# Recurrence by pairs of channel blocks, the merge's rows split behind its first gate, one lasting set of stream buffers, and no gather steps at three borders

## Chip, cores and metric

One core of a Trainium2 chip runs the whole program. The metric is the device time of one execution in microseconds (us); a smaller one is better.

## What is computed

One decoder layer for 512 prompt tokens and 8 x 4 sample tokens, 544 columns in all, 2048 channels, everything in float32:

```python
proj = rmsnorm(x) @ w_in                       # q, k, v, indexer, xb, yb, memory queries
o_attn = attend(top-k keys of an indexer)       # 8 heads
xc = conv_b + sum(shift(xb, j) * conv_w[j])     # width 4, per channel
r = sigmoid(xc_blk @ w_rg + b_rg); i = sigmoid(xc_blk @ w_ig + b_ig)   # 8 blocks of 128 channels
a = exp(-8 * r * softplus(-lam)); u = sqrt(1 - a*a) * (i * xc)
h[t] = a[t] * h[t-1] + u[t]; o_lru = h * gelu(yb)
o_mem = attend(256 memory tokens)               # 4 heads
x = x + sum_n(sigmoid(xn @ w_gate[n]) * (o_n @ w_br[n])) @ w_o
x = x + PEER(rmsnorm(x))    # 16384 one-neuron experts: 8 heads, the best 16 of 128 x 128 keys each
y = rmsnorm(x)
```

## The kernel before, in words

**Matmuls in three parts.** Weights stay in DRAM and stream in chunks of 512 KB. `stream` (L239) loads one with a SyncE DMA (L242) into a buffer `raw`, ScalarE casts it to `hi` and VectorE forms `lo = raw - hi` (`split`, L221 to L223). `project` (L257) multiplies 8 k-blocks of a chunk as hi x hi, hi x lo and lo x hi: 48 matmuls of L272 for 16 k-blocks. The ring holds 3 buffers each of raw, hi and lo in pool `st`; `widen(stack, raw, hl, side)` (L230) opens a further pool with more of them for as long as that stack is open.

**Order.** The program is written out by hand; the build orders each engine's instructions by their place in it, those inside `urgent()` 3000 places ahead, among the ones it takes to be ready. Every engine, and SyncE with its DMAs, then works in that order. Side work is written as generators in four queues (`bg`, `bg2`, `bg3`, `bg4`). Each k-block of a projection calls `pump` once, which adds `rate / 8` steps to each queue's account and takes whole steps from its first generator up to the next `yield`. `drain` takes all that are left.

**Stages.** Prompt and sample tokens are worked off in two parts: part 0 has 288 columns (`xF`), part 1 has 256 (`xA`). `branches(part)` (L391) projects with `w_in` and runs attention heads (`bg2`), memory heads (`bg`) and the recurrence (`bg4`). `merge` (L926) follows, then `output_proj` (L968). Part 0 goes first; `pairs` (L1165) then finds the experts of its tokens, `branches(1)`, `merge`, `output_proj` and `pairs` follow for part 1, then `up` (L1316) for 128 blocks of experts, gate matrices (L1328) beside some of them, and `down` (L1453) with the remaining `up`s. All through this, `bg3` gathers single expert rows for 224 tokens by indirect DMAs on POOL (L1195) and works on them in VectorE (L1243, L1251): one step a row of 128 x 2048 floats, 448 rows, 472 steps in all.

**The recurrence.** `lru(c, xb, late)` (L738) handles block c of 8. Its yields: conv (POOL copies, 4 VectorE operations on part 1); the r gate (weights, matmul L766, sigmoid L768); the i gate; tanh (L773), exp (L775), two VectorE operations and sqrt (L778); the product on POOL (L780), VectorE and the scan (L792); and, once `late` holds the y-branch projection, gelu (L799), product (L800) and the store to `o_dram` (L801). Apart from the gate weights, with two, every tile of it has one buffer. L908 to L911 projects xb of block c, queues the generator, and projects yb. `staged` (L429) copies a projection into one of five `stage` buffers.

**Merge.** For each branch n (memory, attention, recurrence), 8 tiles of `o_dram` are loaded as `oraw` (L940) and split into `oh`, `ol` (L941); then 16 gates (L945) and, two behind, 16 branch projections (L953). `oraw` and the gates' sigmoids `sg` share four buffers of one tag. Gate results wait in PSUM (`ps_p`, four tiles).

**Memory.** SBUF is filled by two stacks, left and right. In part 1 the branch pools lie on the right, under `xA`: `keep` (kT, vN and others, 10.8 KiB a partition by its tiles' shapes), `stage` 5, `ap` 3.5, `lr` 9.1, `bc` (attention), `mp` (memory heads). At L1292 a set of two raw, hi and lo (24 KiB) is opened on the right in place of `keep`, `stage`, `ap` and part of `lr`; it is closed after the merge, opened anew at L1299 for `output_proj`, closed, and opened again at L1309 beside `rp2`. A tile placed on another one's memory waits until that is done with.

Of the kernel before, what the change touches and what calls it, by code (L numbers as in the profile page):

```python
# [176 lines left out]
def program(tc, ins, outs):  # L177
# [213 lines left out]
    def branches(part):  # L391
# [346 lines left out]
        def lru(c, xb, late):  # L738
            def v(i):
                return vec[:, i + c:i + c + 1]  # L740

            xp = lp.tile([128, 3 + HB], F, name="xp")
            if first:
                nc.gpsimd.memset(xp[:, :3], 0.0)
            else:
                nc.gpsimd.tensor_copy(xp[:, :3], tail[:, c])
            nc.gpsimd.tensor_copy(xp[:, 3:], xb[:, p0:])
            xc = lp.tile([128, n_], F, name="xc")
            convs = [(xc[:, p0:], lambda j: xp[:, j:j + HB])]
            if first:  # L750
                nc.gpsimd.tensor_copy(tail[:, c], xp[:, HB:])
                xs = lp.tile([128, NB, 3 + NT], F, name="xs")
                nc.gpsimd.tensor_copy(xs[:, :, :3], scv[:, c])
                nc.gpsimd.tensor_copy(xs[:, :, 3:], bt(xb))
                convs.append((bt(xc), lambda j: xs[:, :, j:j + NT]))
            for dst, src in convs:
                nc.vector.tensor_scalar(dst, src(0), v(V_CW), v(V_CB), op0=OP.mult, op1=OP.add)
                for j in range(1, 4):
                    nc.vector.scalar_tensor_tensor(dst, src(j), v(V_CW + 8 * j), dst, op0=OP.mult, op1=OP.add)
            yield  # L760
            gates = []
            for name, bcol in (("w_rg", V_BR), ("w_ig", V_BI)):
                w = lp.tile([128, 128], F, name=name, bufs=2)
                nc.sync.dma_start(w, ins[name][:, c])
                p = ps_w.tile([128, 512], F, name="w1")
                nc.tensor.matmul(p[:, :n_], w, xc, start=True, stop=True)  # L766
                g = lp.tile([128, n_], F, name=f"g{bcol}")
                nc.scalar.activation(g, p[:, :n_], AF.Sigmoid, bias=v(bcol))  # L768
                gates.append(g)
                yield  # L770
            rg, ig = gates
            th = lp.tile([128, n_], F, name="th")
            nc.scalar.activation(th, rg, AF.Tanh, scale=la[:, 1, c:c + 1])  # L773
            av = lp.tile([128, n_], F, name="av")
            nc.scalar.activation(av, rg, AF.Exp, scale=la[:, 0, c:c + 1])  # L775
            nc.vector.tensor_tensor(rg, av, av, op=OP.mult)
            nc.vector.scalar_tensor_tensor(th, rg, 1.0, th, op0=OP.add, op1=OP.mult)
            nc.scalar.activation(th, th, AF.Sqrt)  # L778
            yield
            nc.gpsimd.tensor_tensor(ig, ig, xc, op=OP.mult)  # L780
            nc.vector.tensor_tensor(th, th, ig, op=OP.mult)
            t0 = lp.tile([128, NB], F, name="t0")
            if first:
                nc.vector.tensor_tensor(t0, bt(av)[:, :, 0], slr[:, c], op=OP.mult)
                nc.vector.tensor_tensor(bt(th)[:, :, 0], bt(th)[:, :, 0], t0, op=OP.add)
                nc.vector.memset(av[:, 0:P0 + 1:NT], 0.0)
            else:
                nc.vector.tensor_tensor(t0[:, :1], av[:, :1], hl[:, c, 0:1], op=OP.mult)
                nc.vector.tensor_tensor(th[:, :1], th[:, :1], t0[:, :1], op=OP.add)
                nc.vector.memset(av[:, :1], 0.0)  # L790
            hs = lp.tile([128, n_], F, name="hs")
            nc.vector.tensor_tensor_scan(hs, av, th, 0.0, op0=OP.mult, op1=OP.add)  # L792
            nc.gpsimd.tensor_copy(hl[:, c, 0:1], hs[:, n_ - 1:])
            if first:
                nc.gpsimd.tensor_copy(hl[:, c, 1:], bt(hs)[:, :, NT - 1])
            yield
            while not late:
                yield
            nc.scalar.activation(ig, late[0], AF.Gelu_apprx_tanh)  # L799
            nc.vector.tensor_tensor(ig, hs, ig, op=OP.mult)  # L800
            nc.sync.dma_start(o_dram[8 + c, :, cols], ig)  # L801
            yield
# [98 lines left out]
        bg4.rate = 2.2  # L901
# [6 lines left out]
        for c in range(8):  # L908
            late = []
            bg4.add(lru(c, staged(CH_XB + c), late))  # L910
            late.append(staged(CH_YB + c))  # L911
# [14 lines left out]
    def merge(c0, x, mp_, side):  # L926
# [41 lines left out]
    def output_proj(c0, mo, xg, o0, rs, sums=None):  # L968
# [6 lines left out]
        for d in range(ND):  # L975
            xr = wp.tile([128, n_], F, name="xr", bufs=2)
# [322 lines left out]
    widen(wide, 2, 2, "right")  # L1299
# [5 lines left out]
    wide.close()  # L1305
# [3 lines left out]
    widen(rps, 2, 2)  # L1309
# [100 lines left out]
    rps.close()  # L1410
    ras = ExitStack()
# [7 lines left out]
    for j in ups:  # L1419
        if j < AHEAD_UP - 3:  # L1420
            up(j)
# [50 lines left out]
    for g in range(16):  # L1472
        bg3.rate = 0.52 if 8 * g < AHEAD_UP else 0.72
# [63 lines left out]
```

## Time and profile before

| | us |
|---|---|
| median of three runs (4437.32 to 4449.01) | 4448.33 |
| the profiled execution: its own time | 4444.03 |
| its span, first to last instruction | 4442.3 |
| TensorE (PE) busy in the span | 4168.0, 94% |
| VectorE (DVE) busy | 3442.7, 77% |
| ScalarE (ACT) busy | 1931.7, 43% |
| GpSimd (POOL) busy | 1210.8, 27% |

PE carries the span. What can be gained lies in the time in which PE waits or runs at a lower clock, and that is bunched at a few places, so the profile is read by stretches. The granted clock is given as a share of full speed (1.00 is 2.4 GHz, 0.50 is 1.2 GHz).

### The profile page before, as it was taken

How to read it: one execution, taken by the hardware profiler on the slowest of the kernel's cores; microseconds unless marked ns; L12 is line 12 of the kernel's file. 1: busy time of each engine (PE TensorE's matmuls, PEld its weight loads, DVE VectorE, ACT ScalarE, POOL GpSimd, SP SyncE). 2: the span in 40 equal slices, each digit the busy share in tenths (PEclk: the TensorE clock that was granted, in tenths of full speed). 3: DMA queues.
4: the chain of work that ended last, by engine and by line, in shares of the span. 5: the costliest groups of instructions: out<-in, count | busy, mean ns of one | idle time of the engine just before them, and what ended most of it. 6: DMA issues, size and time to landing. Idle time of an engine off the chain costs nothing.

```text
span 4442.3 us, 75719 instructions
## 1 busy us (share of the span) xinstructions
PE 4168.0 (94%) x29283; PEld 3990.3 (90%) x29283; DVE 3442.7 (77%) x5243; ACT 1931.7 (43%) x2941; POOL 1210.8 (27%) x1287
## 2 busy tenths in 40 slices
PE   8999999999989877899889889979999999999997
PEld 7868789999976866899889889979999999999997
DVE  6447544455788987798888899978887999997997
ACT  6434753344433348444443358723333333333333
POOL 3022410001244222244332332212222333322333
PEclk9999999999998988899999999999999999999999
DMA  8666545556645776899997679999987999997995
GB/s 265 219 203 214 166 147 173 163 175 189 187 147 173 257 273 215 309 382 378 364 339 243 224 252 364 350 354 348 351 297 265 375 371 380 374 382 261 399 381 190
DMA packets 383562, 1232.82 MB, mean 278 GB/s; under 512 B 51552, under 2 KB 169056, under 8 KB 322272
## 3 DMA queue, kind: packets, MB, share of 16 engines
q1 hardware_dynamic: 314592, 747.69, 49.5%
q0 software_dynamic: 68608, 480.28, 28.2%
q8 instruction: 230, 3.77, 0.3%
q14 instruction: 132, 1.08, 0.1%
HBM read 1167.50 MB, written 60.22 MB: 276 GB/s over the span
## 4 chain that ended last, share of the span: by engine, by line
PE 47%; DVE 9%; DMA 4%; issue 3%; ACT 1%; POOL 1%; DVEq 0%; SPq 0%; ACTq 0%; POOLq 0%
PE mm L272 25%; PE mm L1462 19%; DVE lo L223 3%; PE w L1360 2%; DVE gacc L1251 2%; DVE row L1243 1%; DMA row<-in_vn,idx 1%; DMA x2r<-x_dram 1%; DMA gl<-ge_dram 1%; DMA row<-in_un,idx 1%; POOL cand L1103 0%; DMA raw<-in_u 0%; DMA xnat<-xn_dram 0%; DMA raw<-in_w_in 0%; ACT hi L222 0%
## 5 line engine op out<-in xcount | busy, mean ns | idle before, releaser
L222 ACT CAST hi<-raw 128x1024 fp32r<-128x1024 f32 x1140 | 1192.1, 1050 | 1586.1 <-PE mm L272 796.6
L223 DVE TENSOR_TENSOR lo<-raw,hi 128x1024 fp32r<-128x1024 f32 x1140 | 1426.0, 1254 | 404.3 <-ACT hi L222 394.4
L272 PE MATMUL mm<-xgd,hi 128*128 128x320 f32 (+1 forms) x4608 | 1021.5, 310 | 18.5 <-ACT hi L222 9.9
L272 PEld LDWEIGHTS mm<-xgd,hi 128*128 128x128 f32 x4608 | 773.3, 190 | 19.6 <-ACT hi L222 10.4
L272 PE MATMUL mm<-xgd,lo 128*128 128x320 f32 (+1 forms) x2304 | 715.6, 311 | 28.2 <-DVE lo L223 28.1
L1462 PE MATMUL mm<-zh,hi 128*128 128x320 f32 x2048 | 633.8, 310 | 16.0 <-ACT zh L222 14.7
L1462 PE MATMUL mm<-zh,lo 128*128 128x320 f32 x2048 | 635.0, 310 | 8.9 <-DVE lo L223 8.8
L1462 PE MATMUL mm<-zl,hi 128*128 128x320 f32 x2048 | 634.3, 310 | 1.0 <-DVE zl L223 1.0
L272 PE MATMUL mm<-xF,hi 128*128 128x288 f32 x2976 | 625.5, 303 | 2.1 <-ACT stage L426 2.1
L1195 POOL DMA_INDIRECT row<-in_un,idx x224 | 354.8, 1584 | 902.1 <-PE mm L272 274.3
L1195 POOL DMA_INDIRECT row<-in_vn,idx x224 | 358.5, 1600 | 789.4 <-PE mm L272 266.5
L272 PE MATMUL mm<-xA,hi 128*128 128x256 f32 x2976 | 552.2, 287 | 18.9 <-ACT hi L222 18.9
L1251 DVE SCALAR_TENSOR_TENSOR gacc<-row,hv,gacc 128x2048 f32<-128x2048 f32 x221 | 523.8, 2370 | 49.7 <-DMA row<-in_vn,idx 27.6
L1243 DVE SCALAR_TENSOR_TENSOR row<-row,xnat 128x2048 f32<-128x2048 f32 x224 | 514.9, 2299 | 46.3 <-DMA row<-in_un,idx 23.9
L272 PEld LDWEIGHTS mm<-xA,hi 128*128 128x128 f32 x2976 | 465.8, 192 | 46.0 <-issue 24.6
L272 PEld LDWEIGHTS mm<-xF,hi 128*128 128x128 f32 x2976 | 486.8, 191 | 21.8 <-issue 16.9
L272 PEld LDWEIGHTS mm<-xgd,lo 128*128 128x128 f32 x2304 | 438.1, 190 | 34.8 <-DVE lo L223 34.7
L272 PE MATMUL mm<-xF,lo 128*128 128x288 f32 x1488 | 448.7, 302 | 0.2 <-DVE lo L223 0.2
L272 PE MATMUL mm<-xA,lo 128*128 128x256 f32 x1488 | 428.0, 288 | 13.1 <-DVE lo L223 12.9
L1462 PEld LDWEIGHTS mm<-zh,hi 128*128 128x128 f32 x2048 | 386.1, 189 | 17.3 <-ACT zh L222 15.3
L1462 PEld LDWEIGHTS mm<-zh,lo 128*128 128x128 f32 x2048 | 386.3, 189 | 11.1 <-DVE lo L223 11.1
L1462 PEld LDWEIGHTS mm<-zl,hi 128*128 128x128 f32 x2048 | 386.4, 189 | 1.8 <-DVE zl L223 1.5
(375 smaller groups left out, 6343.6 us busy)
## 6 DMA issues: line engine op xcount, KB each, us to landing
raw<-in_u SPq DMA_DIRECT2D x256, 512.0 KB, 7.8
raw<-in_v SPq DMA_DIRECT2D x256, 512.0 KB, 6.9
raw<-in_w_gate SPq DMA_DIRECT2D x192, 512.0 KB, 4.7
raw<-in_w_in SPq DMA_DIRECT2D x180, 512.0 KB, 4.8
raw<-in_w_br SPq DMA_DIRECT2D x96, 512.0 KB, 4.4
raw<-in_w_o SPq DMA_DIRECT2D x64, 512.0 KB, 4.9
raw<-in_w_pq SPq DMA_DIRECT2D x64, 512.0 KB, 4.3
g_dram<-gs SPq DMA_DIRECT2D x10, 2048.0 KB, 11.8
```

The lines of the kernel that those rows point to most:

```text
L222: nc.scalar.copy(hi, src)
L223: eng.tensor_tensor(lo, src, hi.bitcast(F), op=OP.subtract)
L272: last["mm"] = nc.tensor.matmul(p[:, i, :n], a[:, s], chunk(b[which], u + k), start=(u + k == 0 and pr == 0), stop=(u + k == k_chunks - 1 ...
L1195: i = nc.gpsimd.indirect_dma_start(out=r, out_offset=None, in_=ins[table], in_offset=bass.IndirectOffsetOnAxis(ap=ind[:, s:s + 1], axis=0))
L1243: j = nc.vector.scalar_tensor_tensor(r, r, 1.0, xn, op0=OP.mult, op1=OP.mult, accum_out=h)
L1251: j = nc.vector.scalar_tensor_tensor(acc, r, h, acc, op0=OP.mult, op1=OP.add)
L1360: nc.tensor.matmul(p.rearrange("p (i t) -> p i t", t=4)[:, :, j], o2[:, j], o1[:, j], start=True, stop=True)
L1462: last["mm"] = nc.tensor.matmul(p[:, 0, :NTA], a[:, s], b, start=(k == 0 and pr == 0), stop=(k == 7 and pr == 2))
```

## The change

Five edits. (1) `lru` takes two neighbouring channel blocks at a time: tiles have two halves, per-channel operations come twice, operations without per-channel scalars (L776, L777, L778, L780, L781, L800) come once on both halves, weights and results move with one DMA for both. Conv has one yield for each block, the others one for the pair; a pair waits until both of its yb are there. `bg4.rate` goes from 2.2 to 1.9. (2) In `merge`, the first branch's eight `oraw` are written behind gate 0 instead of ahead of it. (3) The extra set of two raw, hi and lo is opened once, on the left, ahead of pool `ma`, and stays until L1410. (4) `bg3` takes no step during the last four blocks of the second `output_proj` nor beside the `up`s of g = 0; its rates in the `down` stage go from 0.52 and 0.72 to 0.56 and 0.74. (5) Five `up`s instead of three are kept back for g = 0.

```diff
         def lru(c, xb, late):
...
+            xp, xc = tiled("xp", 3 + HB), tiled("xc", n_)
...
+            for i in two:
+                nc.gpsimd.tensor_copy(xp[:, i, 3:], xb[i][:, p0:])
+                convs = [(xc[:, i, p0:], lambda j, i=i: xp[:, i, j:j + HB])]
...
+                for dst, src in convs:
+                    nc.vector.tensor_scalar(dst, src(0), v(V_CW, i), v(V_CB, i), op0=OP.mult, op1=OP.add)
+                    for j in range(1, 4):
+                        nc.vector.scalar_tensor_tensor(dst, src(j), v(V_CW + 8 * j, i), dst, op0=OP.mult, op1=OP.add)
+                yield
             gates = []
             for name, bcol in (("w_rg", V_BR), ("w_ig", V_BI)):
-                w = lp.tile([128, 128], F, name=name, bufs=2)
-                nc.sync.dma_start(w, ins[name][:, c])
-                p = ps_w.tile([128, 512], F, name="w1")
-                nc.tensor.matmul(p[:, :n_], w, xc, start=True, stop=True)
-                g = lp.tile([128, n_], F, name=f"g{bcol}")
-                nc.scalar.activation(g, p[:, :n_], AF.Sigmoid, bias=v(bcol))
+                w = lp.tile([128, 2, 128], F, name=name)
+                nc.sync.dma_start(w, ins[name][:, c:c + 2])
+                g = tiled(f"g{bcol}", n_)
+                for i in two:
+                    p = ps_w.tile([128, 512], F, name="w1")
+                    nc.tensor.matmul(p[:, :n_], w[:, i], xc[:, i], start=True, stop=True)
+                    nc.scalar.activation(g[:, i], p[:, :n_], AF.Sigmoid, bias=v(bcol, i))
                 gates.append(g)
                 yield
             rg, ig = gates
-            th = lp.tile([128, n_], F, name="th")
-            nc.scalar.activation(th, rg, AF.Tanh, scale=la[:, 1, c:c + 1])
-            av = lp.tile([128, n_], F, name="av")
-            nc.scalar.activation(av, rg, AF.Exp, scale=la[:, 0, c:c + 1])
+            th, av = tiled("th", n_), tiled("av", n_)
+            for i in two:
+                nc.scalar.activation(th[:, i], rg[:, i], AF.Tanh, scale=la[:, 1, c + i:c + i + 1])
+            for i in two:
+                nc.scalar.activation(av[:, i], rg[:, i], AF.Exp, scale=la[:, 0, c + i:c + i + 1])
             nc.vector.tensor_tensor(rg, av, av, op=OP.mult)
             nc.vector.scalar_tensor_tensor(th, rg, 1.0, th, op0=OP.add, op1=OP.mult)
             nc.scalar.activation(th, th, AF.Sqrt)
             yield
             nc.gpsimd.tensor_tensor(ig, ig, xc, op=OP.mult)
             nc.vector.tensor_tensor(th, th, ig, op=OP.mult)
...
+            hs = tiled("hs", n_)
+            for i in two:
+                nc.vector.tensor_tensor_scan(hs[:, i], av[:, i], th[:, i], 0.0, op0=OP.mult, op1=OP.add)
...
-            while not late:
-                yield
-            nc.scalar.activation(ig, late[0], AF.Gelu_apprx_tanh)
+            yield
+            while len(late) < 2:
+                yield
+            for i in two:
+                nc.scalar.activation(ig[:, i], late[i], AF.Gelu_apprx_tanh)
             nc.vector.tensor_tensor(ig, hs, ig, op=OP.mult)
-            nc.sync.dma_start(o_dram[8 + c, :, cols], ig)
+            nc.sync.dma_start(o_dram[8 + c:10 + c, :, cols].rearrange("c p n -> p c n"), ig)
             yield
...
-        bg4.rate = 2.2
+        bg4.rate = 1.9
...
-        for c in range(8):
+        for c in range(0, 8, 2):
             late = []
-            bg4.add(lru(c, staged(CH_XB + c), late))
-            late.append(staged(CH_YB + c))
+            bg4.add(lru(c, [staged(CH_XB + c), staged(CH_XB + c + 1)], late))
+            for i in range(2):
+                late.append(staged(CH_YB + c + i))
...
-            with urgent():
-                for k in range(8):
-                    raw = op_.tile([128, n_], F, name="oraw", tag="sg", bufs=4)
-                    nc.sync.dma_start(raw, o_dram[8 * n + k, :, c0:c0 + n_])
-                    split(op[0][k], op[1][k], raw)
+
+            def load():
+                with urgent():
+                    for k in range(8):
+                        raw = op_.tile([128, n_], F, name="oraw", tag="sg", bufs=4)
+                        nc.sync.dma_start(raw, o_dram[8 * n + k, :, c0:c0 + n_])
+                        split(op[0][k], op[1][k], raw)
+
+            if i:
+                load()
             sgs = {}
             for d in range(ND + GLAG):
+                if d == 1 and i == 0:
+                    load()
...
+            if c0 and d == 12:
+                bg3.rate = 0.0
             xr = wp.tile([128, n_], F, name="xr", bufs=2)
...
     branches(1)
     kps.close()
+    widen(wide, 2, 2)
     mas = ExitStack()
     map_ = pool("ma", mas)
     bg3.rate = 0.53
-    widen(wide, 2, 2, "right")
     mA = merge(HA, xA, map_, "left")
-    wide.close()
     big.close()
...
-    widen(wide, 2, 2, "right")
...
-    wide.close()
     mas.close()
     rps = ExitStack()
     rp = pool("rp2", rps)
-    widen(rps, 2, 2)
...
     rps.close()
+    wide.close()
...
-        if j < AHEAD_UP - 3:
+        if j < AHEAD_UP - 5:
             up(j)
...
-        bg3.rate = 0.52 if 8 * g < AHEAD_UP else 0.72
+        bg3.rate = 0.56 if 8 * g < AHEAD_UP else 0.74
...
         if g == 0:
-            for j in range(AHEAD_UP - 3, AHEAD_UP):
+            bg3.rate = 0.0
+            for j in range(AHEAD_UP - 5, AHEAD_UP):
                 up(j)
+            bg3.rate = 0.56
```

## Rows read from the trace of the kernel before

**Rows 1.** The page, part 1: busy time, share and instructions of each engine.

```profile
PE 4168.0 (94%) x29283; PEld 3990.3 (90%) x29283; DVE 3442.7 (77%) x5243; ACT 1931.7 (43%) x2941; POOL 1210.8 (27%) x1287
```

**Rows 2.** Busy time by stretch: window, length, engines, PEclk, DMA share, GB/s.

```profile
410.00:597.00 187.00, 174.93 (x1080) 142.31 (x1078) 94.72 (x251) 123.62 (x191) 71.50 (x104) 0.95 0.54 160
...
1745.00:1797.00 52.00, 15.39 (x44) 10.51 (x44) 19.03 (x57) 38.31 (x52) 3.63 (x10) 0.60 0.22 62
1797.00:2202.00 405.00, 403.29 (x3384) 402.59 (x3384) 365.12 (x344) 185.09 (x238) 159.77 (x99) 0.99 0.97 373
...
2320.00:2345.00 25.00, 11.09 (x50) 9.57 (x49) 14.41 (x17) 8.08 (x12) 3.15 (x2) 0.59 0.87 303
...
2890.00:2942.00 52.00, 28.51 (x162) 26.55 (x162) 31.54 (x33) 11.97 (x18) 8.43 (x7) 0.84 1.04 389
...
3404.00:4330.00 926.00, 923.66 (x6292) 921.38 (x6291) 844.68 (x905) 338.37 (x423) 293.68 (x195) 1.00 0.96 365
```

**Rows 3.** Timeline of PE: start, length, instruction, [idle before it, what ended that].

```profile
1762.21 1.08 PE L834 MATMUL w<-cst,ex 128*128 128x128 f32 x4 [5.09 <-DVE ex L457]
...
1775.94 1.19 PE L766 MATMUL w<-xc,w_rg 128*128 128x256 f32 x2 [7.20 <-issue]
...
1796.88 0.79 PE L272 MATMUL mm<-xA,hi 128*128 128x256 f32 x2 [18.90 <-ACT hi L222]
...
2214.50 0.58 PE L272 MATMUL mm<-mh,hi 128*128 128x256 f32 x1 [12.98 <-ACT hi L222]
...
2329.92 0.58 PE L272 MATMUL mm<-xgd,hi 128*128 128x256 f32 x1 [7.98 <-ACT xgd L295]
...
2339.30 1.33 PE L272 MATMUL mm<-xgd,hi 128*128 128x320 f32 x4 [4.93 <-ACT hi L222]
...
2939.36 1.17 PE L1462 MATMUL mm<-zh,hi 128*128 128x320 f32 x3 [12.04 <-ACT zh L222]
```

**Rows 4.** Timeline of ScalarE (ACT) at the casts ahead of three of these.

```profile
2213.40 1.04 ACT L222 CAST hi<-raw 128x1024 fp32r<-128x1024 f32 x1 [5.29 <-DMA raw<-in_w_o]
...
2328.41 1.04 ACT L222 CAST hi<-raw 128x1024 fp32r<-128x1024 f32 x1 [8.40 <-DMA raw<-in_u]
...
2938.85 0.46 ACT L222 CAST zh<-gl 128x320 fp32r<-128x320 f32 x1 [14.17 <-DVE gl L1447]
```

**Rows 5.** ScalarE's groups from 1600 to 1800: busy us, mean ns | idle before.

```profile
L768 ACT ACT_TABLE_LOAD x13 | 16.7, 1283 | 0.2
L778 ACT ACT_TABLE_LOAD x8 | 10.3, 1283 | 0.1
L799 ACT ACT_TABLE_LOAD x7 | 9.0, 1283 | 1.1 <-DVE th L781 1.0
...
L775 ACT ACT_TABLE_LOAD x6 | 7.7, 1283 | 0.0
```

**Rows 6.** Timeline of VectorE (DVE) at four of its operations.

```profile
582.67 0.64 DVE L800 TENSOR_TENSOR g<-hs,g 128x288 f32<-128x288 f32 x1
...
1777.26 0.42 DVE L800 TENSOR_TENSOR g<-hs,g 128x256 f32<-128x256 f32 x1 [0.63 <-ACT g L799]
...
1786.64 0.42 DVE L800 TENSOR_TENSOR g<-hs,g 128x256 f32<-128x256 f32 x1 [0.31 <-ACT g L799]
...
2323.47 0.42 DVE L981 TENSOR_TENSOR x<-mm,xr 128x256 f32<-128x256 f32 x1
```

**Rows 7.** Instructions on tile xA up to 1790, PE: count, duration in ns.

```profile
L272 PE MATMUL mm<-xA,hi x1488: 274/281/687, 1294.8 to 1738.2; 128*128 128x256 f32 x186
L272 PE MATMUL mm<-xA,lo x744: 274/281/684, 1295.1 to 1738.3; 128*128 128x256 f32 x186
```

**Rows 8.** Timeline of SyncE's DMA issues (SPq) at the end of the second branches.

```profile
1787.71 1.83 SPq L940 DMA_DIRECT2D oraw<-o_dram x4
```

**Rows 9.** ScalarE's waits from 3400 to 4000: us in total, times, longest.

```profile
ACT hi L222 <- PE mm L1462: 178.8, 74, 11.3
```

**Rows 10.** Timeline of POOL at the recurrence's copy of block 5, part 0.

```profile
505.57 0.49 POOL L747 COPY xp<-stage 128x256 f32<-128x256 f32 x1
```

More of the change, by code (lines that the diff above doesn't have):

```diff
@@ L738, in lru, with v, tiled, btj @@
         def lru(c, xb, late):
-            def v(i):
-                return vec[:, i + c:i + c + 1]
-            xp = lp.tile([128, 3 + HB], F, name="xp")
+            two = range(2)
+            def v(i, j):
+                return vec[:, i + c + j:i + c + j + 1]
+            def tiled(name, n):
+                return lp.tile([128, 2, n], F, name=name)
+            def btj(a):
+                return a[:, :, :P0].rearrange("p j (b t) -> p j b t", b=NB)
+            xp, xc = tiled("xp", 3 + HB), tiled("xc", n_)
@@ L743, in lru @@
             if first:
-                nc.gpsimd.memset(xp[:, :3], 0.0)
-            else:
[L746 to L759, printed above, removed]
-            yield
+                nc.gpsimd.memset(xp[:, :, :3], 0.0)
+                xs = lp.tile([128, 2, NB, 3 + NT], F, name="xs")
+            else:
+                nc.gpsimd.tensor_copy(xp[:, :, :3], tail[:, c:c + 2])
@@ new lines, in lru @@
+            for i in two:
+                nc.gpsimd.tensor_copy(xp[:, i, 3:], xb[i][:, p0:])
+                convs = [(xc[:, i, p0:], lambda j, i=i: xp[:, i, j:j + HB])]
+                if first:
+                    nc.gpsimd.tensor_copy(tail[:, c + i], xp[:, i, HB:])
+                    nc.gpsimd.tensor_copy(xs[:, i, :, :3], scv[:, c + i])
+                    nc.gpsimd.tensor_copy(xs[:, i, :, 3:], bt(xb[i]))
+                    convs.append((bt(xc[:, i]), lambda j, i=i: xs[:, i, :, j:j + NT]))
+                for dst, src in convs:
[3 more added lines that the diff above has]
+                yield
@@ L781, in lru @@
             nc.vector.tensor_tensor(th, th, ig, op=OP.mult)
-            t0 = lp.tile([128, NB], F, name="t0")
             if first:
-                nc.vector.tensor_tensor(t0, bt(av)[:, :, 0], slr[:, c], op=OP.mult)
-                nc.vector.tensor_tensor(bt(th)[:, :, 0], bt(th)[:, :, 0], t0, op=OP.add)
-                nc.vector.memset(av[:, 0:P0 + 1:NT], 0.0)
-            else:
-                nc.vector.tensor_tensor(t0[:, :1], av[:, :1], hl[:, c, 0:1], op=OP.mult)
-                nc.vector.tensor_tensor(th[:, :1], th[:, :1], t0[:, :1], op=OP.add)
-                nc.vector.memset(av[:, :1], 0.0)
@@ L791, in lru @@
-            hs = lp.tile([128, n_], F, name="hs")
-            nc.vector.tensor_tensor_scan(hs, av, th, 0.0, op0=OP.mult, op1=OP.add)
-            nc.gpsimd.tensor_copy(hl[:, c, 0:1], hs[:, n_ - 1:])
+                t0 = lp.tile([128, 2, NB], F, name="t0")
+                nc.vector.tensor_tensor(t0, btj(av)[:, :, :, 0], slr[:, c:c + 2], op=OP.mult)
+                nc.vector.tensor_tensor(btj(th)[:, :, :, 0], btj(th)[:, :, :, 0], t0, op=OP.add)
+                for i in two:
+                    nc.vector.memset(av[:, i, 0:P0 + 1:NT], 0.0)
+            else:
+                t0 = lp.tile([128, 2, 1], F, name="t0")
+                nc.vector.tensor_tensor(t0, av[:, :, :1], hl[:, c:c + 2, 0:1], op=OP.mult)
+                nc.vector.tensor_tensor(th[:, :, :1], th[:, :, :1], t0, op=OP.add)
+                for i in two:
+                    nc.vector.memset(av[:, i, :1], 0.0)
@@ L794, in lru @@
+            hs = tiled("hs", n_)
+            for i in two:
+                nc.vector.tensor_tensor_scan(hs[:, i], av[:, i], th[:, i], 0.0, op0=OP.mult, op1=OP.add)
+            nc.gpsimd.tensor_copy(hl[:, c:c + 2, 0:1], hs[:, :, n_ - 1:])
             if first:
-                nc.gpsimd.tensor_copy(hl[:, c, 1:], bt(hs)[:, :, NT - 1])
+                nc.gpsimd.tensor_copy(hl[:, c:c + 2, 1:], btj(hs)[:, :, :, NT - 1])
             yield
-            while not late:
+            while len(late) < 2:
@@ L798, in lru @@
                 yield
-            nc.scalar.activation(ig, late[0], AF.Gelu_apprx_tanh)
+            for i in two:
+                nc.scalar.activation(ig[:, i], late[i], AF.Gelu_apprx_tanh)
             nc.vector.tensor_tensor(ig, hs, ig, op=OP.mult)
-            nc.sync.dma_start(o_dram[8 + c, :, cols], ig)
+            nc.sync.dma_start(o_dram[8 + c:10 + c, :, cols].rearrange("c p n -> p c n"), ig)
             yield
```

## Prediction

> **What bounds the kernel.** The page's first part comes first: PE is busy for 4168.0 of 4442.3 us, the next engine for 3442.7 [rows 1]. Read alone this says that 274 us are left, not where. So I cut the span into stretches and asked for busy time and clock of each [rows 2]. Four kinds are to be seen. In the merge of part 1 PE is busy for 403.29 of 405 us, in the long `down` part for 923.66 of 926: nothing can be won there but by less work, and the change takes none away. At the end of the second `branches`, 1745 to 1797, PE is busy for 15.39 of 52 us at a granted clock of 0.60. At 2320 to 2345 it is busy for 11.09 of 25 at 0.59, and at 2890 to 2942 for 28.51 of 52. Part 0's recurrence (410 to 597) has 12.1 us idle in 187.
>
> PE's timeline then tells what ended the gaps [rows 3]: 5.09, 7.20 and 18.90 us at the drain, 12.98 ahead of the first `w_o` matmul, 7.98 and 4.93 behind the last one, 12.04 at the first `down`. The long ones end on ScalarE's cast of a weight chunk, or on `zh`. ScalarE's timeline goes one step back [rows 4]: the casts had waited 5.29 us for `w_o`, 8.40 for `u`, and `zh` 14.17 for VectorE's product of a loaded `gl`. So these are late transfers, not slow arithmetic.
>
> The profiled execution took 4444.03 us, 0.1% under the median of 4448.33. The sum is made against 4444.0.
>
> **1a. The recurrence by pairs, part 1.** ScalarE's groups between 1600 and 1800 show 13 + 8 + 7 + 6 = 34 table loads on the recurrence's own lines, 1.283 us each [rows 5]. Half of the 34 go, 21.8 us of ScalarE. What that is on the path is read from the last two blocks, which run with no projection left beside them: their products L800 are 9.4 us apart [rows 6]. Five loads are 6.4 of that, 3.0 are left for everything else. A pair costs 6.4 + 2 x 3.0 = 12.4 where two blocks cost 18.8, so 6.4 for each of four pairs, 25.6 in all. From above 25.6; from below 0, if the attention heads set the end of the drain. I take 20, near the upper end, as PE's gap of 7.20 ends on the recurrence's own matmul and only the 5.09 ahead of it on a head's softmax [rows 3]. The pair's single buffers serialise nothing new, as the tiles had one buffer before.
>
> **1b. What moves with it.** Steps: 28 instead of 48, and 256 pumps at 1.9 / 8 give 61, so the lower rate starves nothing. SyncE has half as many loads of gate weights and stores; POOL's product doubles, and a row gather queued behind it on POOL starts under 1.5 us later, which the two rows in flight cover; without that cover VectorE's row operation, and then only it, would start later. The new wait (both yb) has nothing queued behind it in `bg4` but the next pair; it holds up to four of the five `stage` buffers. Part 0: PE's idle 12.1 us there [rows 2] bound the gain; I take 0, with 8 either way for the order of PE's instructions.
>
> **2. Rows behind the first gate, buffers on the left.** By 1790 PE had done 1488 + 744 = 2232 matmuls on `xA` [rows 7]. The 45 channels of `w_in` need 2160, so only 72 were gates: one and a half. The ring's two extra buffers lie where `kT`, `stage`, `ap` and `lr` are live, so the fourth chunk of every five waits for the drain; and SyncE reached the first `oraw` at 1787.71, one us after the last product L800 at 1786.64 [rows 6, 8]. On the left the extra buffers replace `rp`, closed long before, and a piece of the memory heads' pool. PSUM holds four gates, so 2.5 more, at 48 x 403.29 / 3384 = 5.7 us each [rows 2], may run while the drain lasts: 14.2 us at most, 0 at least. The oh and ol tiles now lie on the recurrence's and `stage`'s memory, so the rows themselves are not split sooner after the drain's end. I take two gates, 11 us, as a `sg` buffer comes free only after all eight rows. With 1a that is 31; both upper ends together, 39.8, are more than the stretch's idle 36.6, which is the cap.
>
> **3. Merge to `w_o`.** The cast of the first `w_o` chunk no longer waits for memory. Late next is the merge's last product with its split. The first project meets that piece as its last k-block, 45 matmuls in. From 12.98 idle I take 10; bounds 5 and 13.
>
> **4. `w_o` to `query`.** No set is opened anew here, so `u` can be loaded ahead; and without gather steps in the last four blocks the operation that ended at 2323.47 no longer queues behind gather products [rows 6]. Of 7.98 + 4.93 I take 10; bounds 3 and 13. What stays is the chain from the last `w_o` to `xgd`.
>
> **5. Two more `up`s kept back.** They are moved, not added: 2 x 48 matmuls at 923.66 / 6292 = 0.147 us [rows 2], 14.1 us of cover, while `gl` and `acc` are loaded. With their four chunk loads they pass the gate-matrix steps: 20 `up`s x 16 pumps x 2.8 / 8 = 112 steps of 116, so four are drained. Of 23.5 idle [rows 2] I take 11; bounds 0 and 14.
>
> **6. Gather steps: 0.** Taken out: 64 pumps x 0.53 / 8 = 4.2, 48 x 0.52 / 8 = 3.1, and two `up`s at 0.85, 3.4; 10.7. Put in: 1024 pumps x 0.04 / 8 = 5.1 and 2272 x 0.02 / 8 = 5.7; 10.8. By the same count 469.5 of 472 steps are taken before the end in both kernels. What hides the moved ones is VectorE's free time, 926 - 844.68 us [rows 2], and the 178.8 us of 600 in which ScalarE's casts wait for `down`'s matmuls, not for a transfer [rows 9]. If that cover is gone, each row of 1.05 MB costs its transfer at 365 GB/s, 2.9 us: 31 us.
>
> Sum: 31 + 10 + 10 + 11 = 62; 4444.0 - 62 = **4382**.
>
> **Rivals.** *The heads set the drain.* 1a gives 0, the rest holds: 4402. For it: a PE gap at 1762 ends on a head's exp [rows 3]. Against: 7.20 and 18.90 behind that.
> *Data, not buffers, set the borders.* Parts 3 to 5 give 11 instead of 31: the edit to the ring then does not do what it is for. 4402. For it: 12.04 ended on `gl`, which no ring holds.
> *All four bunches go.* 36.6 + 12.98 + 12.9 + 14: 4368, and with half-clock time behind each gap given back some 14 more: 4354.
> *Transfers are the bound of `down`.* The stretch moves 365 GB/s at 0.96 of the DMA engines [rows 2]; then the moved rows cost 31 us: 4413. Against: casts wait for PE [rows 9]. The Trainium skill ("DMA: Bandwidth & Descriptors", Specifications) puts the HBM limit of one core at some 358 GB/s, by which this part is already at its bound; the trace shows 365 with PE busy for 99.7% of the stretch, so it does not agree that more must be paid.
> *Stage buffers run out in part 0: slower.* The first yb of a pair is held until its gelu, and the buffer is wanted six projections after the second xb; 187 us for 16 projections [rows 2] make that 70 us. One block took 77 us from its copy at 505.57 to its product at 582.67 [rows 6, 10]; a pair by 12.4 / 9.4 of that takes 102. Past 70 us PE stands: 30 us for each of three pairs, 90 in all, 4472. Against: those 77 us are stretched by the sample heads on PE, which stretch the projections as well.
>
> **Chances.** Forecast 0.45, heads 0.20, data 0.12, all gone 0.08, transfers 0.08, stage 0.07. The likeliest, 4382, has its own range of 4362 to 4405 from the bounds of its terms. The range takes in heads, data and transfers and most of the open upper side: 4352 to 4425. A measurement here can tell some 0.3%, 13 us, from no change. Faster by more than that: all cases but the last and the unlucky ends of three, 0.88; within it 0.05; slower 0.07.
>
> **What would show it.** About 17 loads on the recurrence's lines between 1600 and 1800, and a last product near 1760. Four gates done before the first branch matmul. Idle ahead of `w_o` under 4 us, around the last one under 4, at the first `down` under 13. PE still full after that, at some 370 GB/s. Wrong if the last product stays near 1787, if a new gap of over 15 us opens in PE, or if rows are left behind the last matmul.

## The result, and the profile after

The changed kernel took 4415.36 us in the median of five runs (4401.52 to 4417.1), where the kernel before took 4449.01 in the median of five beside it: a ratio of 0.9925, 95% interval 0.9907 to 0.9943. That is 33.7 us less where 62 were forecast: the right direction, inside the range, but 33 us above the predicted 4382. The profiled execution took 4413.15 us, with a span of 4411.4.

The first part of the page answers to [rows 1]:

```profile
PE 4166.7 (94%) x29283; PEld 3988.9 (90%) x29283; DVE 3431.3 (78%) x5195; ACT 1880.0 (43%) x2895; POOL 1203.6 (27%) x1259
```

PE's work is the same 29283 instructions. ScalarE has lost 51.7 us, 46 instructions fewer. The stretches come next; the last four are shifted to where the same work now lies (columns as in [rows 2]):

```profile
410.00:597.00 187.00, 169.33 (x1055) 135.66 (x1055) 91.03 (x236) 107.33 (x180) 69.72 (x91) 0.94 0.51 155
1745.00:1806.00 61.00, 28.50 (x117) 21.48 (x115) 29.14 (x62) 32.67 (x51) 5.06 (x7) 0.70 0.36 123
1806.00:2205.00 399.00, 397.10 (x3315) 395.37 (x3316) 356.65 (x340) 181.59 (x236) 161.04 (x97) 0.99 0.97 371
2310.00:2340.00 30.00, 30.00 (x232) 29.95 (x231) 24.60 (x39) 17.42 (x23) 2.38 (x2) 1.00 0.94 325
2845.00:2932.00 87.00, 75.74 (x482) 73.29 (x481) 58.77 (x77) 30.46 (x42) 9.20 (x8) 0.94 0.99 353
3404.00:4330.00 926.00, 919.52 (x6243) 917.51 (x6243) 854.10 (x913) 334.75 (x422) 287.17 (x200) 1.00 0.97 371
```

The border behind the last `w_o` (2310 to 2340) has no idle left, where PE stood for 13.9 of 25 us. Around the first `down` (2845 to 2932) 11.3 us are idle for 23.5. The end of the second `branches` is another matter: before, PE was busy for 15.39 of 52 us; now it is busy for 28.50 of 61. More work was put into this stretch, the drain, in which the side work that is left is finished, and it became longer. The `down` stretch moves 371 GB/s with PE busy for 919.52 of 926. PE's timeline shows the drain and the border to `w_o`, and answers to [rows 3]:

```profile
1716.67 1.92 PE L777 MATMUL w<-xc,w_rg 128*128 128x256 f32 x4
...
1749.05 3.33 PE L857 MATMUL w<-pT,vN 128*128 128x256 f32 x8
...
1765.63 1.91 PE L777 MATMUL w<-xc,w_rg 128*128 128x256 f32 x4
1767.34 2.64 PE L857 MATMUL w<-pT,vN 128*128 128x256 f32 x8
...
1776.05 0.84 PE L850 MATMUL w<-cst,ex 128*128 128x128 f32 x3 [4.55 <-DVE ex L457]
...
1782.56 1.09 PE L850 MATMUL w<-cst,ex 128*128 128x128 f32 x4 [3.97 <-DVE ex L457]
1784.33 3.36 PE L857 MATMUL w<-pT,vN 128*128 128x256 f32 x8 [0.68 <-ACT pT L851]
1787.47 1.92 PE L777 MATMUL w<-xc,w_rg 128*128 128x256 f32 x4
...
1806.33 0.58 PE L272 MATMUL mm<-oh,hi 128*128 128x256 f32 x1 [15.83 <-ACT oh L222]
...
2211.28 0.39 PE L272 MATMUL mm<-mh,hi 128*128 128x256 f32 x1 [1.07 <-ACT mh L222]
2213.44 0.58 PE L272 MATMUL mm<-ml,hi 128*128 128x256 f32 x1 [1.77 <-DVE ml L223]
```

The first `w_o` matmuls wait 1.07 and 1.77 us for 12.98. In the drain it is one head after another: transposes of `ex`, products with `vN`, and only behind the last head's (1784.33) the last pair's gates (1787.47). The first matmul of the merge's first branch, called the first branch matmul below, follows at 1806.33; before it came at 1803.00. ScalarE's table loads from 1600 to 1800 answer to [rows 5]:

```profile
L778 ACT ACT_TABLE_LOAD x5 | 6.4, 1283 | 4.4 <-PE w L777 4.3
...
L786 ACT ACT_TABLE_LOAD x4 | 5.1, 1283 | 0.1
L789 ACT ACT_TABLE_LOAD x4 | 5.1, 1283 | 1.8 <-DVE av L804 1.8
L815 ACT ACT_TABLE_LOAD x4 | 5.1, 1283 | 0.1
```

These are 5 + 4 + 4 + 4 = 17 for 34, the number forecast. VectorE's timeline shows the end of the conv of the second and the third pair, and the last product:

```profile
1680.84 0.87 DVE L768 SCALAR_TENSOR_TENSOR xc<-xp,vec,xc 128x256 f32<-128x256 f32 x2
...
1727.48 0.46 DVE L768 SCALAR_TENSOR_TENSOR xc<-xp,vec,xc 128x256 f32<-128x256 f32 x1
...
1800.33 0.70 DVE L816 TENSOR_TENSOR g<-hs,g 128x512 f32<-128x512 f32 x1
```

The second pair's conv ends at 1681.71 and its first gate matmul starts at 1716.67, 35 us later; the third pair's ends at 1727.94 and has its gate at 1765.63, 38 us later. The gates' weights were issued at 1659.21 and 1718.62, and no table is needed between conv and gate. The last product comes at 1800.33 where [rows 6] have 1786.64. So the loads left, and the recurrence did not become faster.

To compare runs whose earlier stages differ by some us, the table gives starts counted from the first matmul on `xA`, worked out from each profiled run's records (1294.81 and 1291.32 us in the first two rows). "Last product" is the last of the recurrence. Such a time repeats to a few us only: in the changed kernel and in gather_on, three_ups and borders_as_before, which differ from it only behind the drain, the first branch matmul comes at 515.0, 511.4, 511.5 and 514.9. The `down` stage took 1486.0 to 1509.1 us in the eleven profiled runs that have the changed kernel's code for it, so single profiles do not settle a difference of some us there.

| | last head's vN | last product | first branch matmul | last branch matmul | first on `xgd` | first `down` |
|---|---|---|---|---|---|---|
| before | 472.1 | 491.8 | 508.2 | 906.4 | 1021.7 | 1625.2 |
| after | 495.9 | 509.0 | 515.0 | 913.3 | 1018.4 | 1604.6 |
| pairs_only | 481.1 | 494.2 | 508.9 | 909.6 | 1025.8 | 1629.5 |
| single_blocks | 492.1 | 512.1 | 517.6 | 915.2 | 1022.9 | 1610.6 |
| heads_early | 467.1 | 503.6 | 509.5 | 908.3 | 1014.4 | 1598.0 |
| before_heads_early | 449.4 | 504.0 | 519.1 | 919.0 | 1039.3 | 1645.6 |
| ring_reopened | 472.0 | 485.1 | 504.4 | 899.9 | 1018.8 | 1611.7 |
| rows_first | 496.0 | 509.1 | 515.1 | 914.1 | 1019.0 | 1604.1 |
| own_psum | 491.5 | 460.5 | 494.4 | 893.0 | 1001.4 | 1584.4 |
| heads_two | 466.5 | 488.1 | 493.9 | 892.9 | 998.9 | 1586.1 |
| own_psum_heads_two | 456.4 | 468.7 | 475.4 | 874.2 | 980.7 | 1565.7 |
| single_own_two | 457.2 | 480.2 | 485.9 | 882.2 | 992.3 | 1579.0 |
| before_heads_two | 482.0 | 501.4 | 517.4 | 918.4 | 1033.8 | 1633.9 |
| own_h17 | 437.4 | 458.6 | 472.8 | 869.8 | 978.6 | 1560.7 |

The span's 30.9 us, stage by stage: 3.5 gained until the first matmul on `xA`, 6.9 lost from there to the last branch matmul, 10.2 gained from that to the first on `xgd`, 17.4 up to the first `down`, 6.2 in `down`, 0.6 behind it. The 6.9 are two things: behind the last product the first branch matmul now follows after 6.0 us for 16.4, but the last product itself comes 17.2 later.

### The profile page after: what moved, and what is told of

Same layout as the page of the kernel before. It is cut to its first block, busy times and chain, and to the rows that moved or that the text cites. A ratio compares the mean times of both kernels' runs of the same rounds, so it can differ in the third digit from the quotient of the medians.

```text
span 4411.4 us, 75518 instructions
## 1 busy us (share of the span) xinstructions
PE 4166.7 (94%) x29283; PEld 3988.9 (90%) x29283; DVE 3431.3 (78%) x5195; ACT 1880.0 (43%) x2895; POOL 1203.6 (27%) x1259
## 5 line engine op out<-in xcount | busy, mean ns | idle before, releaser
L1221 POOL DMA_INDIRECT row<-in_vn,idx x224 | 342.7, 1530 | 851.5 <-PE mm L272 260.1
L1277 DVE SCALAR_TENSOR_TENSOR gacc<-row,hv,gacc 128x2048 f32<-128x2048 f32 x221 | 523.8, 2370 | 27.0 <-DMA row<-in_vn,idx 20.1
```

Source lines behind the costliest of these rows:

```text
L1221: i = nc.gpsimd.indirect_dma_start(out=r, out_offset=None, in_=ins[table], in_offset=bass.IndirectOffsetOnAxis(ap=ind[:, s:s + 1], axis=0))
L1277: j = nc.vector.scalar_tensor_tensor(acc, r, h, acc, op0=OP.mult, op1=OP.add)
```

## The experiments

Ratios are to the kernel before, on the same chip, with 95% intervals; those of different groups are comparable to some 0.2%, the width of the intervals.

### The recurrence and the heads

**pairs_only** is the kernel before with edit 1, **single_blocks** the changed one without it (`lru` and its loop as in the kernel before, rate 2.2). In the other two one line is changed, in the kernel after and in the one before:

```diff
-                    bg2.rate = 1.15
+                    bg2.rate = 1.7
```

> The kernel before with edit 1 alone (recurrence by pairs, rate 1.9). Term 1a of the forecast: last product L800 some 20 us sooner than 1786.64, time 4429, ratio 0.9955. Theory 'heads' (the pairs' bursts push the heads back on TensorE, and the last pair starts only behind the last head): the last head near 1785, the last product near 1800, time 4444 to 4456, ratio 0.999 to 1.002.

> The changed kernel with edit 1 undone (single blocks, rate 2.2), edits 2 to 5 kept. Term 1a: 20 us slower than the changed kernel, 4435. Theory 'heads': the last head is back near 1765, the last product near 1787 or sooner, and the time is within 5 us of the changed kernel or under it, 4405 to 4418.

> The changed kernel with the heads' rate in part 1 at 1.7 for 1.15: their 40 steps are spread over 188 k-blocks in place of 278. Theory 'heads': the last head is done before 1750, the last pair's gates follow the conv, the last product comes before 1775, and the time falls by 20 to 30 us, to 4385 to 4395. Rival 'the recurrence's own chain is the end': the heads are done sooner, the last product stays at 1795 to 1801, and the time is 4410 to 4418.

> The kernel before with the heads' rate in part 1 at 1.7 for 1.15. Theory 'heads': the heads are done before 1750, two single blocks of 9.4 us are left, the last product comes near 1775 for 1786.64, the time falls by some 10 us to 4439, ratio 0.998. Rival 'own chain': last product near 1787, ratio 1.000.

Measured: 0.9989 (0.9977 to 1.0001), 0.9931 (0.9914 to 0.9948), 0.9913 (0.9899 to 0.9928) and 1.0036 (1.0020 to 1.0052). Edit 1 is worth 0 to 10 us alone and 3 on top of the others, with intervals that overlap: term 1a's 20 are not there. Nor are the pairs what made the last product late: with single blocks it comes at 512.1 for 491.8 in the kernel before, so edits 2 to 5 did, and ring_reopened below points to edit 3. But the theory "heads" fell as well, in the form that a later end of the heads is the cause. In heads_early the last head comes 29 us sooner (467.1 for 495.9) and the last product 5 (503.6 for 509.0). In the kernel before, heads 22.7 us sooner (449.4 for 472.1) go with a last product 12.2 later (504.0 for 491.8), and the time grows by 16 us. Heads and recurrence push each other: there, what is put ahead delays the other one. VectorE's last product of heads_early stands where it stood:

```profile
1799.56 0.70 DVE L816 TENSOR_TENSOR g<-hs,g 128x512 f32<-128x512 f32 x1
```

### What ties them

All the heads' products and transposes, the memory heads' and the recurrence's gates take their PSUM tiles from `ps_w`, four tiles that the program hands out in the order in which it was written. A pair's gates take four of them. By the program's text, while a gate waits for its conv, the heads' tiles written behind it can't be had, and the other way round; PE is busy with other matmuls meanwhile, so the trace names no such wait, and runs must show it. **own_psum** gives the gates a tile of their own in part 1, **one_tile** only puts both blocks of a pair into one tile:

```diff
-                    p = ps_w.tile([128, 512], F, name="w1")
-                    nc.tensor.matmul(p[:, :n_], w[:, i], xc[:, i], start=True, stop=True)
+                    if first or i == 0:
+                        p = (ps_w if first else ps_l).tile([128, 512], F, name="w1")
+                    q = p[:, :n_] if first else p[:, i * n_:(i + 1) * n_]
+                    nc.tensor.matmul(q, w[:, i], xc[:, i], start=True, stop=True)
...
+    psC.close()
+    psL = ExitStack()
+    ps_w = pool("ps_w4", psL, 3, space=PSUM)
+    ps_l = pool("ps_l", psL, 1, space=PSUM)
     branches(1)
```

> The changed kernel, but in part 1 the recurrence's gates have a PSUM tile of their own (both blocks of a pair in one) and heads and others have three, where all shared four in the order of the program. Theory 'shared tiles' (each w tile is handed out in program order, so the pair's gates wait for heads and heads for the pair's gates): the gates follow their conv by under 12 us in place of 35, the last product comes before the last head, the drain ends some 10 to 20 us sooner and the time is 4395 to 4405. Rival 'the work of the engines is the bound, whatever the order': the last of heads and recurrence ends near 1790 to 1800 as before, 4410 to 4418.

> The changed kernel, with both blocks of a pair in one PSUM tile for each gate in part 1, 8 tiles for 16, from the same four. Theory 'shared tiles': a shorter line, a gain of 3 to 8 us, 4405 to 4412. Rival 'work of the engines': no difference, 4411 to 4418.

Measured: 0.9899 (0.9882 to 0.9917), 4397.48 us, and 0.9938 (0.9922 to 0.9954). The tile of its own gives some 12 us by the ratios, and the first branch matmul 20.6 us sooner in the table; the packing gives nothing, where 3 to 8 us were expected. With two tiles from the shared four for a pair, one_tile's gates still follow their conv by 33 and 25 us (second and third pair, from its trace): it is the sharing, not the number of tiles. VectorE in own_psum, at the end of the third pair's conv (its second block) and at the last product:

```profile
1690.81 0.48 DVE L768 SCALAR_TENSOR_TENSOR xc<-xp,vec,xc 128x256 f32<-128x256 f32 x1
...
1753.69 0.69 DVE L818 TENSOR_TENSOR g<-hs,g 128x512 f32<-128x512 f32 x1 [0.34 <-ACT g L817]
```

and PE there, at that block's first gate, the last three heads and the first branch matmul:

```profile
1697.95 0.59 PE L779 MATMUL w<-xc,w_rg 128*128 128x256 f32 x2
...
1755.19 3.35 PE L859 MATMUL w<-pT,vN 128*128 128x256 f32 x8 [0.68 <-ACT pT L853]
...
1767.87 3.36 PE L859 MATMUL w<-pT,vN 128*128 128x256 f32 x8 [0.67 <-ACT pT L853]
...
1781.76 3.35 PE L859 MATMUL w<-pT,vN 128*128 128x256 f32 x8 [0.68 <-ACT pT L853]
1787.61 0.58 PE L272 MATMUL mm<-oh,hi 128*128 128x256 f32 x1 [2.50 <-ACT oh L222]
```

The gate follows its conv by 6.7 us (1691.29 to 1697.95) where it took 35 and 38, and the last product is done 47 us sooner. What isn't separated is whether the wait was for the tile itself or for the place that it gave the gate in PE's order; both go with the sharing.

Now the heads alone end the drain: the last three are 12.7 and 13.9 us apart, in the round trips from PE to VectorE to ScalarE and back. That the merge waits for them at all is no matter of data. Its first branch is the memory heads', whose last row was stored long before the first load; SyncE in the changed kernel, and then SyncE's wait for that load in own_psum:

```profile
1657.65 0.38 SPq L500 DMA_DIRECT2D o_dram<-mo  x1
...
1802.13 1.38 SPq L959 DMA_DIRECT2D oraw<-o_dram  x3
```

```profile
SPq L961 <- PE w L859: 13.0, 1, 13.0
```

The load comes 144 us behind that store and 1.1 behind the last product, and in own_psum it waits 13.0 us and is issued at 1785.14, as the last head's `vN` matmuls end (1785.11) and ahead of that head's own store (1786.51). So there, as the trace has it, it waits for memory that the side work still reads. A place of their own, which might take the drain out of the path, wasn't tried.

**heads_two** shortens the heads' round trips in the changed kernel; **own_psum_heads_two** has both edits:

```diff
+            ex = []
...
-                e = soft(bp, lg[:, :nk], mx, ASCALE, "ex", T)
+                ex.append(soft(bp, lg[:, :nk], mx, ASCALE, "ex", T))
                 yield
+            for j, qb in enumerate(qbs):
+                nk = (qb + 1) * 128
                 p = ps_w.tile([128, 512], F, name="w1")
...
-                    nc.tensor.transpose(p[:, k * 128:(k + 1) * 128], e[:, k * 128:(k + 1) * 128], ident)
+                    nc.tensor.transpose(p[:, k * 128:(k + 1) * 128], ex[j][:, k * 128:(k + 1) * 128], ident)
```

> The changed kernel with another order inside a head: both query blocks' products and exps first, then both transposes, so that a head makes two round trips between engines for three. Theory 'shared tiles, handed out in program order': a head holds the line for less time, the last pair's gates come 10 to 20 us sooner, the last product near 1785, 4395 to 4405. Rival 'work of the engines': last product near 1800, 4411 to 4418.

> The recurrence's own PSUM tile and the other order inside a head together. Theory 'shared tiles': heads and recurrence are done before 1765, the first branch matmul follows by 1772 in place of 1806, the idle around the drain falls under 15 us, and the time is 4380 to 4390. Rival 'work of the engines': the same as with the tile alone, first branch matmul near 1788, 4395 to 4400.

Measured: 0.9867 (0.9848 to 0.9886), 4384.01 us, and 0.9824 (0.9802 to 0.9845), 4366.39 us. Both did more than expected; PE is done with heads and recurrence before it is done with the three gates. By the drain heads_two and own_psum are alike (first branch matmul at 493.9 and 494.4); in the profiled runs they part in `down`, 1486.0 for 1505.5 us, whose code neither of them changes. PE of own_psum_heads_two at the last head and at the first branch matmul, the stretch between (columns as above), and its page:

```profile
1742.57 1.68 PE L862 MATMUL w<-pT,vN 128*128 128x256 f32 x8
...
1763.01 0.58 PE L272 MATMUL mm<-oh,hi 128*128 128x256 f32 x1 [11.91 <-ACT oh L222]
```

```profile
1743.00:1764.00 21.00, 9.09 (x69) 8.77 (x68) 13.49 (x20) 11.48 (x15) 5.29 (x4) 0.79 0.86 278
```

```profile
PE 4149.7 (95%) x29283; PEld 3981.7 (91%) x29283; DVE 3432.0 (79%) x5195; ACT 1890.1 (43%) x2905; POOL 1216.5 (28%) x1259
```

The last head lies between matmuls on `xA`, and the first branch matmul comes 39.6 us sooner than after the change (475.4 for 515.0 in the table). What is left is 11.91 us on the split of the first branch's rows.

**single_own_two** is that version with single blocks, **before_heads_two** the kernel before with the heads' edit alone, **own_h17** the version with the heads' rate at 1.7:

> The version with the recurrence's own tile and the other order inside a head, but with single blocks for pairs (edit 1 undone, rate 2.2). If the pairs save what the last two blocks showed (6.4 us for a pair) once nothing else sets the end: last product 6 to 15 us later than 1756, time 4373 to 4382. Rival 'pairs are worth nothing': 4362 to 4370.

> The kernel before with the other order inside a head alone. If heads and shared tiles already set the drain of the kernel before: the last product some 10 us sooner than 1786.64 with two or three blocks left behind the heads, 4432 to 4440, ratio 0.996 to 0.998. Rival 'there the recurrence's own chain of blocks set it': last product near 1787, 4444 to 4451.

> The version with the recurrence's own tile and the other order inside a head, with the heads' rate at 1.7 for 1.15. If heads still end the drain: the last head some 10 us sooner, 4357 to 4363. Rival 'the recurrence or the rows' memory ends it': 4364 to 4370.

Measured, on a chip on which the kernel before took 4475.73 us: 0.9854 (0.9837 to 0.9871), 1.0006 (0.9992 to 1.0021) and 0.9784 (0.9767 to 0.9801), 4379.72 us. The ratios must serve here, the absolute times expected don't hold on that chip. Once the tie is cut, the pairs are worth 10.5 us at the first branch matmul (485.9 against 475.4 in the table, two profiled runs on two chips) and 0.3% in the ratios (0.9854 against 0.9824). So a saving of the kind that 1a saw is there, about half its size, and the shared tiles had taken it. In the kernel before the heads' round trips did not set the end, and its last head came no sooner (482.0 for 472.1); PE of before_heads_two:

```profile
1806.41 3.35 PE L844 MATMUL w<-pT,vN 128*128 128x256 f32 x8 [0.96 <-ACT pT L838]
1809.56 0.76 PE L766 MATMUL w<-xc,w_rg 128*128 128x256 f32 x2
...
1818.08 1.19 PE L766 MATMUL w<-xc,w_rg 128*128 128x256 f32 x2 [7.33 <-issue]
```

Two blocks still follow the last head, 8.5 us apart, with an idle 7.33 between them that answers to the 7.20 of [rows 3]. The rate of 1.7 gives 2.6 us more at the first branch matmul (472.8 for 475.4) by the trace. Its ratio is the best of all, but those 2.6 us are not the 0.4% by which it lies under own_psum_heads_two's, which was taken on another chip; the rest is open.

### Rows, ring and borders

**rows_first** writes the rows ahead of gate 0 again (edit 2 undone). **ring_reopened** opens the extra set on the right, closes and reopens it as before (edit 3 undone):

```diff
-    widen(wide, 2, 2)
...
+    widen(wide, 2, 2, "right")
     mA = merge(HA, xA, map_, "left")
+    wide.close()
...
```

> The changed kernel with edit 2 undone: the first branch's rows are written ahead of gate 0. Term 2 of the forecast: fewer gates beside the drain, 11 us slower, 4422 to 4427. Rival 'gates run beside the drain only put its own matmuls back': the count of gates before the first branch matmul falls from three, and the time is within 4 us, 4410 to 4418.

> The changed kernel with edit 3 undone: the extra raw, hi and lo are opened on the right, closed and opened anew as before. Terms 3 and 4 of the forecast (the late transfers are late for want of a free buffer): the gap of some 13 us ahead of w_o comes back, and 8 to 13 us behind the last one, 4430 to 4437, ratio 0.996 to 0.998. Rival 'data, not buffers': both gaps stay closed, 4411 to 4418, ratio 0.992.

Measured: 0.9929 (0.9911 to 0.9947) and 0.9964 (0.9951 to 0.9977). Edit 2 is worth nothing: the gates before the first branch matmul stay three, and every column of the table is within 1 us of after. Edit 3 is worth 17 us by the ratios, 7 at the first `down` of the table, and PE shows where:

```profile
1763.89 3.35 PE L857 MATMUL w<-pT,vN 128*128 128x256 f32 x8 [0.68 <-ACT pT L851]
...
1788.35 0.79 PE L272 MATMUL mm<-xA,hi 128*128 128x256 f32 x2 [18.74 <-ACT hi L222]
...
2208.18 0.58 PE L272 MATMUL mm<-mh,hi 128*128 128x256 f32 x1 [13.15 <-ACT hi L222]
```

The 13.15 ahead of `w_o` are back, and 7.2 of the 13.9 us around the last one. But ahead of the merge this kernel is the better one: its last head comes 24 us sooner than after the change and its first branch matmul 10.6 (504.4 for 515.0). Both kernels have done 2304 matmuls on `xA` by then. In the changed one the last 72 of these run ahead of the last two heads; here they wait for their chunk, 18.74 us, and run behind them. So gates run in the drain shorten its tail and go with a later end of the chain ahead. They explain a part of that at most: the fifth head's `vN` starts 15.4 us sooner with the ring reopened (412.3 for 427.7), and at that time neither kernel has done the 2160 matmuls that the 45 channels of `w_in` need ahead of the gates. What else in the lasting set holds up the heads is open.

**gather_on** undoes edit 4, **three_ups** edit 5, **borders_as_before** both:

> The changed kernel with edit 4 undone: gather steps run on in the last blocks of w_o and beside the ups of g = 0, at the rates of before. Forecast (part 4 of it by this edit, part 6 nothing): some 5 us of idle come back behind the last w_o, nothing elsewhere, 4418 to 4422. Rival 'the moved steps are paid in the down part': there PE's small gaps, 20.5 us behind the first 40 us of it, fall back to some 13, and that gives the 5 us back, 4411 to 4417.

> The changed kernel with edit 5 undone: three ups kept back for five. Term 5 of the forecast: the gap at the first down, 12 us on the product of a loaded gl, comes back, 11 us slower, 4422 to 4428. Rival 'the quiet gather of edit 4 closed that gap, not the cover': the idle around the first down stays near 11 us, 4411 to 4418.

> The changed kernel with edits 4 and 5 both undone. If either alone closes the gap at the first down: now it comes back, idle around the first down near 24 us for 12, 4425 to 4432. Rival 'the buffers of edit 3 closed it': idle there stays at 12 to 17, 4418 to 4425 as with edit 4 alone undone.

Measured: 0.9954 (0.9936 to 0.9972), 0.9914 (0.9895 to 0.9934) and, on the other chip, 0.9935 (0.9919 to 0.9951). PE of gather_on behind the last `w_o` and ahead of the first `down`:

```profile
2314.95 0.39 PE L272 MATMUL mm<-xgd,hi 128*128 128x256 f32 x1 [1.55 <-DVE xgd L296]
...
2318.42 0.58 PE L272 MATMUL mm<-xgd,hi 128*128 128x256 f32 x1 [2.97 <-ACT xgd L295]
...
2859.89 0.90 PE L272 MATMUL mm<-xgd,hi 128*128 128x320 f32 x2 [6.43 <-ACT hi L222]
```

and of borders_as_before at the first `down`:

```profile
2939.81 1.17 PE L1483 MATMUL mm<-zh,hi 128*128 128x320 f32 x3 [10.48 <-ACT zh L222]
```

Edit 4 is worth 13 us by the ratios: some 5 of it lie behind `w_o`, some 5 at `down`. Edit 5 alone is worth nothing that shows: without it the idle around the first `down` is 12.5 us for 11.3. The gap on `zh` (12.04 in [rows 3]) returns only with both undone, as 10.48; either edit closes it. That gap is not paid in full, though: from the first matmul on `xgd` to the last `down` borders_as_before takes 2094.5 us and gather_on 2096.4, for 2082.7 after. The idle in the rest of `down` is 20.1 us in gather_on and 20.5 after, so the gather's moved steps cost nothing there. It is 14 to 28 us in the twelve profiled runs with five `up`s kept back and 11 to 15 in the six with three, so edit 5 may cost some us; the ratios don't show it.

## Why the prediction was right or wrong

**The failed step is 1a, and 2 with it**: 31 of the 62 us. Every observation under 1a holds. There are 17 loads, and the last pair, alone with the engines, took 13.6 us from its first gate matmul to the end of its product (1787.47 to 1801.03), where the last single block had taken 11.1 (1775.94 to 1787.06). What failed is the step from there to the path: "What that is on the path is read from the last two blocks, which run with no projection left beside them". The time of a block alone was taken for the time of every block. Beside heads a block's time is its place in the line for the four `ps_w` tiles, and half as many loads change next to nothing there: 35 and 38 us pass between conv and gate. "The pair's single buffers serialise nothing new" looked at SBUF alone; in PSUM a pair's gates stand in one line with the heads. The reason for 20 and not 0, that PE's gap of 7.20 ends on the recurrence's own matmul, named the last one in a shared line, not the one that sets its pace. Measured for 20 us: 0 to 10 alone, 10.5 once the line is cut. The Trainium skill ("Perfetto Trace Analysis", Matmuls) wants independent matmul groups to rotate through different PSUM banks. These runs agree only in part: heads and gates did rotate, through four tiles, and it was the shared rotation that tied them (gates 35 and 38 us behind their conv with it, 6.7 with a tile apart).

**Term 2** was right that the gates would go (three before the first branch matmul) and that this shortens the tail: 6.0 us behind the last product for 16.4, 10.4 of the 11 forecast. It was wrong to put the cost ahead of that at nothing: rows_first shows nothing gained by the rows, and ring_reopened that with the lasting set the last head comes 24 us later, of which the gates explain a part. Terms 1a and 2 together: 31 forecast; 6.9 lost between part 1's first matmul and its last branch matmul, and 3.5 gained ahead of that, which neither term speaks of.

**1b**: part 0 is unchanged (first branch matmul at 619.40 for 619.14), as forecast. Its recurrence has 17.7 us idle for 12.1, inside the 8.

**Terms 3 to 5**: 10, 10 and 11 forecast, 31 in all. From the last branch matmul to the first on `xgd` 10.2 were gained, up to and through `down` 23.6, 33.8 in all; 6.2 of these lie in `down`, within what that stage repeats to. Term 3 and the half of 4 that it gives to the buffers are shown by ring_reopened, the other half by gather_on. Of term 5 the size held and the cause did not: the quiet gather of edit 4 does it as well as the cover.

**Term 6** held: 0, and PE stays full.

**The rivals.** *Heads* was nearest to what happened, at 1a = 0, but it names a symptom: heads 29 us sooner brought the first branch matmul 5.5 us sooner, and in the kernel before 10.9 later. *Data, not buffers* fell with ring_reopened. *Transfers* fell: no row is paid for, at 371 GB/s. The Trainium skill ("DMA: Bandwidth & Descriptors", Specifications) gives some 358 GB/s for a core; the trace passes that again. *Stage buffers*: no stall of 30 us in part 0. Of the signs named, the loads came as said, as did the idle at the three borders (2.8, 0 and 11.3 us); the last product did not move to 1760 but to 1800.33, later than the 1787 that was to prove the forecast wrong, and three gates were done, not four. The range of 4362 to 4405 is not what the bounds of the terms add up to: without the 8 either way of 1b, these give 8 to 77 us, 4367 to 4436.

The trace of before had shown it. There, too, gates came behind heads; the end of the third block's conv and its first gate matmul, on VectorE and PE:

```profile
1678.18 0.48 DVE L759 SCALAR_TENSOR_TENSOR xc<-xp,vec,xc 128x256 f32<-128x256 f32 x1
...
1694.46 0.60 PE L766 MATMUL w<-xc,w_rg 128*128 128x256 f32 x2
```

That is 15.8 us, and a gate matmul needs no table. The other blocks of part 1 have 37.0, 11.4, 8.8, 3.8, 7.4 and 7.1 us there, and the last one 0.1: the blocks whose spacing was taken for all end with the only one that did not wait.

## What to carry to other kernels

Work saved on an engine counts in a stage where that engine ends the wait; for a chain that shares tiles with another, look at the time from operand ready to operation start, and at what stands between. A small pool of PSUM tiles shared by two independent chains made one chain of them here: give each its own, and pipeline the round trips inside each, before anything is made shorter. Before work is put into an idle stretch, ask what the stretch waits for, and whether the work delays that: here it shortened the tail by 10 us, and the lasting set that let it in went with a chain that ended 17 later. And ask whether what follows waits for data or only for a place in memory.

## What had not been expected

On one of the chips the kernel before took 4475.73 us in the median of 17 runs, where on others it took 4444.31 to 4449.01. The four kernels profiled there reached their first branch matmul of part 0 at 629 to 652 us, all others at 609 to 621; what is slower there stays open. And the drain's chain itself runs partly at the lower of the clock's two levels: the last head's eight `vN` matmuls took 3.36 us after the change, where PE had stood idle for 3.97 us shortly before and the granted clock from 1784 to 1788 was 0.50, and 1.68 in own_psum_heads_two, where they stand between other matmuls and the granted clock from 1742 to 1745 was 1.00.
